# A hybrid decoder layer on one core: block sums of W_out made by GpSimd early in attention, FF1 weights through GpSimd's queue, and the gate's product as one pass

## The chip, the cores and the metric

The kernel runs on one core of a Trainium2 chip. The metric is the device time of one execution in microseconds (us), lower is better. The kernel before took a median of 2267.89 us in three runs (2264.93 to 2271.97).

## The reference

One decoder layer over 2048 tokens of width 1024, in float32:

```
n = RMSNorm(x)
h = x + W_out [ GLA_heads(n) ; DilatedSWA_heads(n) ]
h = h + SqReLU_MLP(RMSNorm(h))          # FF1: 1024 -> 4096, FF2: 4096 -> 1024
y = RMSNorm_final(h)
```

One input projection W_in makes the queries, keys, values and gates of both mixers. GLA is gated linear attention in chunks, with four heads; its forget gate is a low-rank product, log_sigmoid((n W_low) W_2 + b), where n W_low has 16 columns and W_2 is 16x256. The other mixer is windowed attention with strides 1, 4 and 16 (three branches per head, eight heads), whose branch outputs are combined by their softmax denominators.

## The kernel before, in words

**Products.** TensorE has to give float32 results from the faster form fp32r. So each operand is split into a high part that fp32r holds and the rest, and `mm3` (L139 to L142) issues three matmuls: high by high (L140), low by high (L141), high by low (L142). ScalarE makes the high part (L484) and VectorE the low one (L485) in `split`. The large products are done as 2x2 blocks with seven block products in place of eight (numbers j = 1 to 7), so sums and differences of blocks of each operand are needed.

**Stages.** The trace's 2263 us fall into the input projection in two halves of the tokens (to about 520 us), attention (to about 868), the product with W_out (to about 1040), FF1 (to about 1690) and FF2. The order of the instructions on each engine is fixed when the kernel is built: a scheduler lays out TensorE, VectorE, ScalarE and GpSimd by a simulated timeline, and each engine then runs its list in order. In attention, a plan says with which of some 160 units of work a step is issued (`at_unit`).

**The gate.** `gate` (L304) runs 16 times, once per 128 tokens, inside the input projection. It sets a 17x128 tile to one, transposes the 128x16 product `glow` (L309), copies it in (L310) and multiplies by the 17x256 matrix of W_2 and b in full float32 (L312). The trace shows that product as two matmuls of 17x256 each.

**Sums for W_out.** `mix_wo` (L1112) is called four times in the stage of the W_out product, once per pair of row blocks c and c+4. SyncE's queue loads 2 x 512 KB into `wtraw`, GpSimd makes four differences of 128x512 in place (L1118) and each is split by ScalarE and VectorE into `wb`. Beside this, GpSimd and VectorE combine the last branch outputs of attention (L927 to L950); the result goes into `mT` and from there into TensorE's product (L141 with the tile ps_d). `load_wo` (L1103) loads the unmixed blocks through `woraw`.

**FF1 weights.** There are 32 groups (16 weight blocks for each half of the tokens) with seven block products each. `load_w1` (L1346) loads a group of 1024x256 as two halves of 512 KB into one of two buffers `w1raw`; `prep1` (L1356) makes the block sums on VectorE (L1369 to L1373), splits them into `w1comb` and, once a half was read for the last time, asks for that half of the group two further on. These loads stand on SyncE's queue (L1354), as nearly all transfers do. SyncE issues in order, and each of its transfers also waits for the landing of the one eight before it. Around the first groups its queue also holds the transposed rows that go out and come back (hTD, L1254 and L1291), and the stores hD and actD.

**Other names.** `pt` (L878) is ScalarE's copy of transposed probabilities, which TensorE reads in L890; `ar` (L1472) and `bb` (L1267) are ScalarE's copies of transposes that TensorE waits for in the W_out stage; `gla` tiles belong to GLA, whose step has GpSimd products (L1020 to L1025, L1067) and a ScalarE scaling behind L1067 (L1069); `qp` is a query tile that GpSimd reorders and rounds for strided attention (L804). The only transfers on GpSimd's queue are 16 accumulating loads of 512 KB in FF2 (L1698).

## Time and profile before

| | |
|---|---|
| median of three runs | 2267.89 us |
| the profiled execution | 2265.11 us |
| its span in the trace | 2263.3 us |
| mean granted TensorE clock | 0.995 |
| TensorE busy | 2226.8 us |
| VectorE, ScalarE, GpSimd busy | 1696.3, 1249.3, 503.4 us |
| moved by DMA | 482.80 MB |

The trace is of one execution; the profiled time is 1.8 us above its span, for what lies before the first and after the last instruction. "Busy" counts the time in which at least one instruction of the engine runs. A busy TensorE can still run at half its clock; the column PEclk of a table by stage tells that. Queries by stage give the busy time of each engine between two times; the list of waits gives what an engine waited for last; the chain of waits follows the end of the span back from releaser to releaser.

### The profile page before, as it was taken

How to read it: one execution, taken by the hardware profiler on the slowest of the kernel's cores; microseconds unless marked ns; L12 is line 12 of the kernel's file. 1: busy time of each engine (PE TensorE's matmuls, PEld its weight loads, DVE VectorE, ACT ScalarE, POOL GpSimd, SP SyncE). 2: the span in 40 equal slices, each digit the busy share in tenths (PEclk: the TensorE clock that was granted, in tenths of full speed). 3: DMA queues.
4: the chain of work that ended last, by engine and by line, in shares of the span. 5: the costliest groups of instructions: out<-in, count | busy, mean ns of one | idle time of the engine just before them, and what ended most of it. 6: DMA issues, size and time to landing. Idle time of an engine off the chain costs nothing.

```text
span 2263.3 us, 35306 instructions
## 1 busy us (share of the span) xinstructions
PE 2226.8 (98%) x12436; PEld 1924.6 (85%) x12436; DVE 1696.3 (75%) x3172; ACT 1249.3 (55%) x2483; POOL 503.4 (22%) x471
## 2 busy tenths in 40 slices
PE   9999999999999998999899999999999999999998
PEld 8978998899999997888688888888888888888876
DVE  8788878766677678778777778767686796566788
ACT  6665446535877884456555566555555433333435
POOL 1210002025286676100000000000006322032452
PEclk9999999999999999999999999999999999999999
DMA  6457754786667965768645446554479997676775
GB/s 205 133 182 242 249 163 125 219 250 220 208 210 221 296 191 206 256 220 263 212 131 164 130 158 224 168 168 155 139 251 286 316 301 265 216 254 240 258 262 177
DMA packets 363602, 482.80 MB, mean 213 GB/s; under 512 B 20197, under 2 KB 269558, under 8 KB 353184
## 3 DMA queue, kind: packets, MB, share of 16 engines
q1 hardware_dynamic: 358926, 471.89, 64.0%
q0 software_dynamic: 4352, 8.39, 2.1%
q8 instruction: 98, 1.61, 0.3%
q14 instruction: 80, 0.66, 0.1%
q10 hardware_dynamic: 146, 0.27, 0.0%
HBM read 330.74 MB, written 154.44 MB: 214 GB/s over the span
## 4 chain that ended last, share of the span: by engine, by line
PE 86%; DVE 5%; DMA 4%; issue 3%; POOL 1%; ACT 1%; POOLq 0%; SPq 0%; DVEq 0%; ACTq 0%
PE ps_a L141 8%; PE ps_a L142 8%; PE ps_a L140 8%; PE ps_c L140 7%; PE ps_c L142 7%; PE ps_c L141 7%; PE ps_d L141 4%; PE ps_d L142 4%; PE ps_d L140 4%; PE ps_a L890 4%; PE ps_o L142 4%; PE ps_o L140 4%; PE ps_o L141 4%; PE ps_d L871 3%; PE ps_c L853 2%
## 5 line engine op out<-in xcount | busy, mean ns | idle before, releaser
L1649 POOL TENSOR_TENSOR bs<-bs,rb 128x1024 f32<-128x1024 f32 x60 | 177.4, 2964 | 1025.5 <-DMA actD<-ring 781.6
L485 DVE TENSOR_TENSOR cb<-bs,cb 128x1024 fp32r<-128x1024 f32 x104 | 166.5, 1601 | 137.6 <-ACT cb L484 137.6
L484 ACT ACTIVATE cb<-bs 128x1024 fp32r<-128x1024 f32 x104 | 110.3, 1061 | 287.5 <-issue 151.6
L485 DVE TENSOR_TENSOR w1comb<-w1raw,w1comb 128x512 fp32r<-128x512 f32 x224 | 153.3, 686 | 84.2 <-ACT w1comb L484 84.2
L484 ACT ACTIVATE w1comb<-w1raw 128x512 fp32r<-128x512 f32 x224 | 139.7, 625 | 87.7 <-PE ps_a L142 27.2
L862 ACT ACTIVATE pe<-pe,O 128x256 f32<-128x256 f32 (+1 forms) x384 | 158.0, 454 | 53.7 <-DVE O L861 51.3
L890 PE MATMUL ps_a<-v,pt 128*128 128x65 f32 x1200 | 180.8, 255 | 5.6 <-ACT pt L878 5.6
L890 PEld LDWEIGHTS ps_a<-v,pt 128*128 128x128 f32 x1200 | 176.1, 196 | 7.2 <-ACT pt L878 6.0
L871 PE MATMUL ps_d<-ident,pe 128*128 128x128 f32 x600 | 160.7, 282 | 0.0
L861 DVE CUSTOM_DVE_ANT_0 pe<-ps_c,nb 128x256 f32<-128x256 f32 (+1 forms) x384 | 126.5, 361 | 44.4 <-PE ps_d L871 17.7
L284 ACT ACTIVATE wcomb<-wraw 128x512 fp32r<-128x512 f32 (+2 forms) x119 | 90.0, 757 | 98.7 <-PE ps_a L141 35.1
L140 PE MATMUL ps_c<-hb,w1comb 128*128 128x512 f32 x320 | 124.7, 390 | 2.3 <-DVE acc L1443 1.4
L142 PE MATMUL ps_c<-hb,w1comb 128*128 128x512 f32 x320 | 124.5, 389 | 0.0
L141 PE MATMUL ps_c<-hb,w1comb 128*128 128x512 f32 x320 | 124.5, 389 | 0.0
L142 PE MATMUL ps_c<-cb,ca 128*128 128x512 f32 x312 | 121.8, 391 | 0.0
L141 PE MATMUL ps_c<-cb,ca 128*128 128x512 f32 x312 | 121.7, 390 | 0.0
L140 PE MATMUL ps_c<-cb,ca 128*128 128x512 f32 x312 | 121.6, 390 | 0.0
L485 DVE TENSOR_TENSOR ca<-ra,ca 128x1024 fp32r<-128x1024 f32 x84 | 117.4, 1398 | 0.0
L1428 ACT ACTIVATE acc<-acc 128x512 f32<-128x512 f32 x96 | 60.5, 631 | 90.9 <-DVE acc L1443 42.0
L871 PEld LDWEIGHTS ps_d<-ident,pe 128*128 128x128 f32 x600 | 110.2, 188 | 0.3
L349 POOL TENSOR_TENSOR acc<-acc,misc 128x264 f32<-128x264 f32 (+1 forms) x32 | 38.7, 1222 | 313.7 <-DVE acc L348 300.8
L142 PE MATMUL ps_a<-wcomb,tb 128*128 128x256 f32 (+1 forms) x344 | 97.7, 284 | 0.0
(464 smaller groups left out, 7206.4 us busy)
## 6 DMA issues: line engine op xcount, KB each, us to landing
ra<-actD SPq DMA_DIRECT2D x52, 1024.0 KB, 7.7
actD<-ring SPq DMA_DIRECT2D x176, 256.0 KB, 3.3
rb<-w_ff SPq DMA_DIRECT2D x88, 512.0 KB, 5.9
bs<-w_ff SPq DMA_DIRECT2D x72, 512.0 KB, 5.9
w1raw<-w_ff SPq DMA_DIRECT2D x64, 512.0 KB, 4.3
k<-kD SPq DMA_DIRECT2D x16, 1024.0 KB, 8.1
rb<-hTD SPq DMA_DIRECT2D x28, 512.0 KB, 5.9
wraw<-w_in SPq DMA_DIRECT2D x48, 256.0 KB, 3.4
```

The costliest lines, as they stand in the source:

```text
L140: T.matmul(out, sh, mh, start=first, stop=False, **kw)
L141: T.matmul(out, sl, mh, start=False, stop=False, **kw)
L142: T.matmul(out, sh, ml, start=False, stop=last, **kw)
L284: A.activation(hi, src, AF.Copy, scale=sc)
L484: A.activation(hi, src, AF.Copy)
L485: V.tensor_tensor(lo, src, hi.bitcast(F32), op=OP.subtract)
L861: V.tensor_tensor_reduce(p, s, bias, scale=1.0, scalar=BIG, op0=OP.add, op1=OP.min, accum_out=nm)
L862: A.activation(p, p, AF.Exp, bias=nm, scale=-1.0)
L871: T.transpose(pb[:, i * 128:i * 128 + 128], src, ident)
L890: T.matmul(self.b.opsum[:, n % 4], self.pt[:, i * 128:i * 128 + 128], self.b.v[:, blk, cols], start=first, stop=last)
L1428: A.activation(v, v, AF.Relu)
L1649: (engines or ((G,), (V, V))[len(sums) - 1])[e].tensor_tensor(v, v, r, op=OP.add if op == "+" else OP.subtract)
```

## The change

- **The gate** becomes one fp32r matmul. ScalarE writes the rounded `glow` twice (columns 0 to 15 and 33 to 48), VectorE writes the rest into columns 17 to 32, and columns 16 and 49 hold ones; the 128x50 tile is transposed, copied and multiplied by a 50x256 matrix: rows 0 to 16 the rounded weights, 17 to 32 the same again, 33 to 49 what the rounding left of them. That matrix is made once, ahead of the second half, by a ScalarE and a VectorE instruction and a transfer within SBUF.
- To make room, the gain of the first norm lives in `CX` in the first half; the gains and the gate's weights come later through two small DRAM tiles (`gD`, `wD`): three loads at the start go, eight small transfers come after the second weight loads.
- **`sum_wo`** makes the differences of W_out's blocks in attention: for each c two loads of 512 KB into `wtsum`, four GpSimd subtractions and one store of 1 MB to `wtD`, a step per unit from unit 8 on. `mix_wo` then loads 2 x 512 KB of finished differences and only splits them. 4 MB more are loaded and 4 MB more stored than before.
- **`load_w1`** issues on GpSimd's queue.

The diff, with most context left out (a changed line's number after is up to 29 higher):

```diff
@@ -230,9 +230,12 @@
-    misc = slot("misc")
-    gB, gnB, w2b = misc[:, :D], misc[:, D:D + 512], misc[:17, D + 512:D + 768]
-    gTs = [misc[:17, D + 768 + 128 * i:D + 896 + 128 * i] for i in range(2)]
+    misc = slot("misc", FR)
+    gB, gnB = misc[:, :D].bitcast(F32), misc[:, D:D + 512].bitcast(F32)
+    w2b, w2raw = misc[:50, D + 512:D + 768], misc[:50, D + 768:D + 1024]
+    gTs = [w2raw[:, 128 * i:128 * i + 128] for i in range(2)]
+    small = const.tile([128, 96], F32, name="small")
+    lows = [misc[:, 2 * D:2 * D + 50], small[:, :50].bitcast(FR)]
@@ -258,6 +261,7 @@
+    gD, wD = dram.tile([1, D + 512], F32, name="gD"), dram.tile([17, 256], F32, name="wD")
@@ -303,11 +307,13 @@
     def gate(glow, t):
-        gT = gTs[t % 2]
-        V.memset(gT, 1.0)
+        gT, l = gTs[t % 2], lows[t % 2]
+        hi = bass.AP(tensor=l.tensor, offset=l.offset, ap=[*l.ap[:1], [33, 2], [1, 16]])
+        A.activation(hi, glow[:, None, :].to_broadcast([128, 2, 16]), AF.Copy)
+        V.tensor_tensor(l[:, 17:33], glow, l[:, 0:16].bitcast(F32), op=OP.subtract)
         pt = ps("d")
-        T.transpose(pt[:16, :128], glow, ident)
-        V.tensor_copy(gT[:16], pt[:16, :128])
+        T.transpose(pt[:50, :128], l.bitcast(F32), ident)
+        V.tensor_copy(gT, pt[:50, :128])
         pg = ps("d")[:, :256]
         T.matmul(pg, gT, w2b, start=True, stop=True)
@@ -491,13 +497,13 @@
     def x_stat(t):
-        A.activation(CX[:, :D], xs[t], AF.Square, accum_out=ss)
+        A.activation(c12[:, :D], xs[t], AF.Square, accum_out=ss)
     def x_scale(t, cs=slice(0, D)):
-        V.scalar_tensor_tensor(xs[t][:, cs], xs[t][:, cs], X[t], gB[:, cs], op0=OP.mult, op1=OP.mult)
+        V.scalar_tensor_tensor(xs[t][:, cs], xs[t][:, cs], X[t], CX[:, cs], op0=OP.mult, op1=OP.mult)
@@ -609,7 +615,7 @@
         x_load(0, xs[0])
-        g1, one = c11[:1, :D], c12[:1, :128]
+        g1, one = c11[:1, :D], c21[:1, :128]
@@ -621,18 +627,15 @@
-        SP.dma_start(gnB, bcast_row(a["gla_norm_g"], 512))
-        SP.dma_start(w2b[:16], a["gla_gate_w2"].rearrange("o r k -> (o r) k"))
-        SP.dma_start(w2b[16:17], a["gla_gate_b"])
-        V.tensor_copy(gB[:, :512], gp[0])
+        V.tensor_copy(CX[:, :512], gp[0])
-        A.activation(gB[:, 512:], gp[1], AF.Copy)
+        A.activation(CX[:, 512:D], gp[1], AF.Copy)
@@ -678,6 +681,13 @@
                 load_w(1, n, k)
+        SP.dma_start(gD[:, :D], a["attn_norm_g"])
+        SP.dma_start(gD[:, D:], a["gla_norm_g"])
+        SP.dma_start(wD[:16], a["gla_gate_w2"].rearrange("o r k -> (o r) k"))
+        SP.dma_start(wD[16:], a["gla_gate_b"])
+        SP.dma_start(misc[:, :D + 512].bitcast(F32), bcast_row(gD, D + 512))
+        for r, n in ((0, 17), (17, 16), (33, 17)):
+            SP.dma_start(w2raw[r:r + n].bitcast(F32), wD[:n])
@@ -726,6 +736,11 @@
         taken(1, 2)
+    for l in lows:
+        A.activation(l[:, 16:50:33], pair, AF.Copy, scale=0.0, bias=1.0)
+    A.activation(w2b, w2raw.bitcast(F32), AF.Copy)
+    V.tensor_tensor(w2raw, w2raw.bitcast(F32), w2b.bitcast(F32), op=OP.subtract)
+    SP.dma_start(w2b[33:].bitcast(F32), w2raw[33:].bitcast(F32))
@@ -904,8 +919,6 @@
-    small = const.tile([128, 96], F32, name="small")
     def combine_load(pr, half):
@@ -1108,15 +1121,28 @@
+    wtD = dram.tile([4, 128, 2 * D], F32, name="wtD")
+    def sum_wo(c):
+        raw = slot("wtsum")
+        for k in range(2):
+            SP.dma_start(raw[:, D * k:D * k + D], wo[:, c + 4 * k])
+        yield
+        b11, b12, b21, b22 = [raw[:, 512 * k:512 * k + 512] for k in range(4)]
+        for dst, x, y in ((b12, b12, b11), (b22, b22, b12), (b21, b21, b22), (b11, b22, b11)):
+            G.tensor_tensor(dst, x, y, op=OP.subtract)
+            yield
+        issue_later(4, wtD[c], raw[:, :2 * D])
+        yield
     def mix_wo(c):
         raw = slot("wtraw")
-        SP.dma_start(raw[:, :D], wo[:, c])
-        SP.dma_start(raw[:, D:2 * D], wo[:, c + 4])
-        b11, b12, b21, b22 = [raw[:, 512 * k:512 * k + 512] for k in range(4)]
-        for dst, x, y, j in ((b12, b12, b11, 5), (b22, b22, b12, 6), (b21, b21, b22, 4), (b11, b22, b11, 7)):
-            G.tensor_tensor(dst, x, y, op=OP.subtract)
-            split(*block_view(j, c), dst)
+        for k in range(2):
+            SP.dma_start(raw[:, D * k:D * k + D], wtD[c, :, D * k:D * k + D])
+        for k, j in ((1, 5), (3, 6), (2, 4), (0, 7)):
+            split(*block_view(j, c), raw[:, 512 * k:512 * k + 512])
     for part in range(4):
@@ -1203,6 +1229,9 @@
     NU = len(units)
+    sums_wo = [x for c in range(4) for x in [sum_wo(c)] * 6]
+    for n, x in enumerate(sums_wo):
+        at_unit(8 + AHEAD + n, next, x)
@@ -1351,7 +1380,7 @@
             g0 = g % NP * 256
             for k in halves:
-                SP.dma_start(raw1[g % 2][:, 4 * k:4 * k + 4], w1[:, 4 * k:4 * k + 4, g0:g0 + 256])
+                G.dma_start(raw1[g % 2][:, 4 * k:4 * k + 4], w1[:, 4 * k:4 * k + 4, g0:g0 + 256])

```

Three places of the order of instructions follow.

GpSimd in early attention, before (L1020 to L1025 and L1067 are a GLA step's products, `qp` is reordered for the third head; in the trace this is 576 to 592 us):

```order
L1023 TENSOR_TENSOR gla<-gla 64x2x128 [waits DMAHW2_49,Activation_49]
L1023 TENSOR_TENSOR gla<-gla 64x2x128 [waits Pool_49]
L1025 TENSOR_TENSOR gla<-gla 128x2 [waits Pool_49]
L1020 TENSOR_TENSOR gla<-gla 128x256 [waits Activation_49]
L804 COPY qp<-qs 128x512 [waits DMAHW4_49,PE_49]
L804 COPY qp<-qs 128x512 x3
L1067 TENSOR_TENSOR gla<-gla 128x512 [waits Activation_49]
L758 MEMSET v 128x16x2 [waits PE_49]
```

And after (L1134 are the subtractions on `wtsum`, L1080 is what L1067 was, L1036 what L1023 was, L819 what L804 was):

```order
L1134 TENSOR_TENSOR wtsum<-wtsum 128x512
L1036 TENSOR_TENSOR gla<-gla 64x2x128 [waits DMAHW2_49,Activation_49]
L1036 TENSOR_TENSOR gla<-gla 64x2x128 [waits Pool_49]
L1038 TENSOR_TENSOR gla<-gla 128x2 [waits Pool_49]
L1033 TENSOR_TENSOR gla<-gla 128x256 [waits DMAHW3_49,PE_49,Activation_49]
L1134 TENSOR_TENSOR wtsum<-wtsum 128x512 [waits DMAHW3_49,PE_49]
L819 COPY qp<-qs 128x512 [waits DMAHW1_49,PE_49]
L819 COPY qp<-qs 128x512 x3
L1080 TENSOR_TENSOR gla<-gla 128x512 [waits Activation_49]
L773 MEMSET v 128x16x2 [waits DMAHW4_49]
L1134 TENSOR_TENSOR wtsum<-wtsum 128x512 [waits DMAHW5_49,Pool_49]
```

One subtraction with a wait for its load stands ahead of a reordering of `qp` and of the GLA product behind it; twelve others stand shortly ahead of these rows.

GpSimd at the end of attention, before (L948 and L950 are the combination of the last branch outputs, L1118 the subtractions for W_out; 876 to 923 us):

```order
L942 TENSOR_TENSOR gla<-gla 128x8 [waits DVE_49]
L942 TENSOR_TENSOR gla<-gla 128x8 x2
L948 TENSOR_TENSOR O_9446<-O_9446,gla 128x4x128 [waits Pool_49]
L948 TENSOR_TENSOR cmb<-cmb,gla 128x4x128 [waits Pool_49] x2
L950 TENSOR_TENSOR O_9446<-O_9446,cmb 128x4x128 [waits Pool_49] x2
L1118 TENSOR_TENSOR wtraw<-wtraw 128x512 [waits DMAHW6_49,PE_49]
L1118 TENSOR_TENSOR wtraw<-wtraw 128x512 [waits DMAHW7_49,Pool_49]
L1118 TENSOR_TENSOR wtraw<-wtraw 128x512 [waits Pool_49]
L1118 TENSOR_TENSOR wtraw<-wtraw 128x512
L1118 TENSOR_TENSOR wtraw<-wtraw 128x512 [waits DMAHW2_49,Activation_49]
```

And after (L961 and L963 are L948 and L950):

```order
L955 TENSOR_TENSOR gla<-gla 128x8 [waits DVE_49]
L955 TENSOR_TENSOR gla<-gla 128x8 x2
L961 TENSOR_TENSOR O_9507<-O_9507,gla 128x4x128 [waits Pool_49]
L961 TENSOR_TENSOR cmb<-cmb,gla 128x4x128 [waits Pool_49] x2
L963 TENSOR_TENSOR O_9507<-O_9507,cmb 128x4x128 [waits Pool_49] x2
L1383 DMA w1raw<-w_ff 128x4x256 [waits PE_49]
L1383 DMA w1raw<-w_ff 128x4x256
L1383 DMA w1raw<-w_ff 128x4x256 [waits PE_49]
L1383 DMA w1raw<-w_ff 128x4x256
L1383 DMA w1raw<-w_ff 128x4x256 [waits DMASW0_49,DVE_49]
```

Behind the last combination stand no more subtractions, but the loads of FF1 weights, all 64 of them one after the other.

VectorE at the start of FF1, before (`w1raw_11392` is the buffer of the even groups, `w1raw_11541` that of the odd ones; `acc1` and L1443, L1447 are sums of products; L1274 to L1277 serve the second half's norm; L1369 is the first sum of a new group, 1092 to 1107 us):

```order
L1443 TENSOR_TENSOR acc1_11548<-ps_a_11549,acc1_11548 128x512
L485 TENSOR_TENSOR w1comb_11515<-w1raw_11392,w1comb_11515 128x512
L1276 TENSOR_TENSOR xh_11250<-bb_9974,xh_11250 128x512
L1277 TENSOR_TENSOR xh_11250<-xh_11250,bb_9974 128x512
L485 TENSOR_TENSOR w1comb_11515<-w1raw_11541,w1comb_11515 128x512
L1443 TENSOR_TENSOR acc1_11651<-ps_d_11652,acc1_11651 128x512
L1369 TENSOR_TENSOR w1raw_11392<-w1raw_11392 128x4x128
L485 TENSOR_TENSOR w1comb_11516<-w1raw_11392,w1comb_11516 128x512
L1447 TENSOR_TENSOR acc1_11548<-ps_c_11672,xs1_11547 128x512
```

And after (`w1raw_11437` even, `w1raw_11586` odd; L1398 is what L1369 was, L1472 and L1476 what L1443 and L1447 were):

```order
L1472 TENSOR_TENSOR acc1_11593<-ps_a_11594,acc1_11593 128x512
L491 TENSOR_TENSOR w1comb_11560<-w1raw_11437,w1comb_11560 128x512
L1472 TENSOR_TENSOR acc1_11696<-ps_d_11697,acc1_11696 128x512
L491 TENSOR_TENSOR w1comb_11561<-w1raw_11437,w1comb_11561 128x512
L1430 TENSOR_TENSOR ring1_11858<-acc1_11593 128x256 x2
L1398 TENSOR_TENSOR w1raw_11437<-w1raw_11437 128x4x128
L1430 TENSOR_TENSOR ring1_11858<-acc1_11593,ring1_11858 128x256
L1476 TENSOR_TENSOR acc1_11593<-ps_c_11717,xs1_11592 128x512
L491 TENSOR_TENSOR w1comb_11561<-w1raw_11437,w1comb_11561 128x512
L1399 TENSOR_TENSOR w1raw_11437<-w1raw_11437 128x4x128
```

The split of the new group's first block (`w1comb_11516`, after `w1comb_11561`) moves from behind the first sum to ahead of it; the last reading of the even buffer's old contents (`w1comb_11515` and `w1comb_11560` from the even buffer) stays ahead of both.

## The prediction

> **What bounds the kernel now.** The profiled execution took 2265.11 us, 2263.3 of them in the trace, and it is the base of the sum; the median of three runs is 2.8 us above it. Read first is the page's first part, busy time by engine, and then the table by stage (for each stretch: its length, busy time of each engine, granted TensorE clock, DMA share, GB/s).
>
> ```profile
> PE 2226.8 (98%) x12436; PEld 1924.6 (85%) x12436; DVE 1696.3 (75%) x3172; ACT 1249.3 (55%) x2483; POOL 503.4 (22%) x471
> ...
> 57.00:510.00 453.00, 452.62 (x2766) 398.03 (x2765) 349.22 (x548) 238.96 (x468) 52.58 (x45) 1.00 0.64 195
> ...
> 566.00:623.00 57.00, 57.00 (x518) 56.18 (x518) 39.81 (x172) 46.20 (x144) 15.74 (x26) 1.00 0.69 209
> ...
> 850.00:906.00 56.00, 49.51 (x285) 42.55 (x284) 48.98 (x89) 25.44 (x62) 37.01 (x42) 0.94 0.57 201
> ...
> 1076.00:1133.00 57.00, 50.41 (x218) 39.29 (x217) 40.48 (x74) 29.86 (x53) 0.00 (x0) 1.00 0.65 207
> 1133.00:2100.00 967.00, 967.00 (x4268) 800.72 (x4267) 711.43 (x1081) 489.01 (x724) 126.30 (x53) 1.00 0.65 209
> ```
>
> TensorE is the bound: it idles 36.5 us in all, and in the two long stretches 57 to 510 and 1133 to 2100 less than 0.4 us. So an edit pays in two ways only: it takes work off TensorE where it never waits, or it fills one of the holes, of which 850 to 906 (6.5 us) and 1076 to 1133 (6.6 us) are the largest the change can reach. Time saved on another engine elsewhere is worth nothing. What TensorE waited for in 850 to 930, by the list of waits, and then one hole as the chain of waits shows it:
>
> ```profile
> PE ps_d L141 <- DVE mT L485: 3.3, 1, 3.3
> PE ps_a L890 <- ACT pt L878: 3.2, 1, 3.2
> PE ps_c L1337 <- ACT ar L1472: 1.7, 1, 1.7
> ```
>
> ```profile
> 890.27 0.69 PE ps_d L141
> 890.96 0.43 PE ps_d L142
> ...
> 893.52 0.43 PE ps_d L142
> 893.95 0.23 PE ps_d L140
> ```
>
> The second view shows that a long hole costs twice. After the 3.3 us wait the product's matmuls take 0.43 us each, against 0.23 later; eight of them at 0.20 more make 1.6 us. The table's clock of 0.94 in that stage is the same thing.
>
> **The gate.** Before, two full float32 passes; in the chain (a stage where TensorE is always on it) and, for the form the change uses, two consecutive fp32r matmuls of 256 columns on TensorE's timeline:
>
> ```profile
> 112.04 0.62 PE ps_d L312 x2
> ```
>
> ```profile
> 59.73 0.28 PE L141 MATMUL ps_a<-wcomb,tb 128*128 128x256 f32 x1
> 59.85 0.29 PE L142 MATMUL ps_a<-wcomb,tb 128*128 128x256 f32 x1
> ```
>
> Starts lie 0.12 us apart, and the 256 columns are what TensorE passes, whatever the number of rows. One gate falls from 0.62 to 0.12, 16 of them by 16 x 0.50 = 8.0 us. The transpose stays one instruction. The added ScalarE copy of 128x32 and VectorE subtraction of 128x16 lie under TensorE, with VectorE busy 349 of 453 us there; without that cover they would be 32 short instructions of 0.2 to 0.3 us, some 8 us. I take **-8.0**, with ends -7 and -9.5 (the passage into and out of float32 may cost a little too).
>
> The moved gains and the eight small transfers are issued behind the second weight loads, well before the first gate at 112; the start loses three loads. I cost these at 0, hidden under TensorE's work in 57 to 510, with 1 us either way for the start.
>
> **The subtractions leave the W_out stage.** The 3.3 us hole ends when VectorE has combined the last outputs and split `mT`. Its timeline just before, and GpSimd's:
>
> ```profile
> 880.82 0.16 DVE L936 TENSOR_TENSOR gla<-gla,cmb 128x8 f32<-128x8 f32 x1
> 881.02 1.25 DVE L937 TENSOR_TENSOR gla<-gla 128x8 f32<-128x8 f32 x1
> 882.30 1.21 DVE L936 TENSOR_TENSOR gla<-gla,cmb 128x8 f32<-128x8 f32 x1
> ...
> 884.97 0.68 DVE L948 TENSOR_TENSOR O<-O,gla 128x512 f32<-128x512 f32 x1
> 885.57 3.45 DVE L948 TENSOR_TENSOR cmb<-cmb,gla 128x512 f32<-128x512 f32 x2
> ```
>
> ```profile
> 879.57 2.67 POOL L950 TENSOR_TENSOR O<-O,cmb 128x512 f32<-128x512 f32 x2
> 882.19 6.28 POOL L1118 TENSOR_TENSOR wtraw<-wtraw 128x512 f32<-128x512 f32 x4
> ```
>
> The same VectorE instruction (L936) takes 0.16 us at 880.82 and 1.21 at 882.30, and the two products of L948 take 3.45 us where one alone takes 0.68. Each long one overlaps a GpSimd instruction. With the four subtractions of 882.19 to 888.47 gone, VectorE saves 1.21 - 0.16 = 1.05 and 3.45 - 1.36 = 2.09, together 3.1 of the 3.3 us, and the slow matmuls behind the hole go too, since a hole of a few tenths brings none. Full value 3.3 + 1.6 = 4.9. I take **-4.5**; ends 0 (if the combination's own GpSimd instructions now fall there) and -5.2.
>
> The 1.7 us wait for `ar` stands behind the last four splits on ScalarE. GpSimd begins the subtractions when the second half has landed, and ScalarE's last split and its copy follow their end:
>
> ```profile
> 918.15 5.68 POOL L1118 TENSOR_TENSOR wtraw<-wtraw 128x512 f32<-128x512 f32 x3 [0.79 <-DMA wtraw<-w_out]
> ```
>
> ```profile
> 923.86 0.63 ACT L484 ACTIVATE wb<-wtraw 128x512 fp32r<-128x512 f32 x1 [1.06 <-POOL wtraw L1118]
> 924.40 1.55 ACT L1472 ACTIVATE ar<-ps_c 128x512 f32<-128x512 f32 x3
> ```
>
> From that landing, 918.1, four splits of 0.63 would be done by about 920.7, so the wait is over before it begins: **-1.7**, ends 0 and -2. The other hole, behind `pt` (3.2 us), is ScalarE waiting for `woraw`, which the change does not touch. It stays; ScalarE now has four splits ahead of the last `pt`, and I leave 1 us either way in the range.
>
> **The subtractions enter early attention.** GpSimd is idle there for most of the time (15.7 of 57 us busy), and 16 subtractions of 1.3 to 2.2 us are some 28 us. But its list is in order: one subtraction now waits for a load of `wtsum`, and behind it stand a `qp` reordering for the third head and a GLA product that ScalarE's list needs. SyncE's list has become longer by eight loads and four stores, and the stores wait for GpSimd. In the trace of before:
>
> ```profile
> 578.61 3.98 POOL L804 CAST qp<-qs 128x512 fp32r<-128x512 f32 x4
> 583.98 1.28 POOL L1067 TENSOR_TENSOR gla<-gla 128x512 f32<-128x512 f32 x1 [1.38 <-ACT gla L1054]
> ```
>
> ```profile
> 586.23 1.27 ACT L1069 ACTIVATE gla<-gla,stats 128x128 f32<-128x128 f32 x4
> ```
>
> ```profile
> 598.83 0.23 PE L851 MATMUL ps_c<-k,qp 128*128 128x128 f32 x1
> ```
>
> ScalarE uses the GLA product at 586.2, 1 us after it is there; `qp` of the third head is used from 598.8. The order is built for the new place: ScalarE's use stands behind three `pt` copies more than before. What remains is that loads are late in a crowded stretch. I take **+1**; ends 0 and +8 (a wait as long as the 3.3 us hole plus its slow matmuls, 4.9, and one smaller).
>
> **FF1 weights on GpSimd's queue.** From the list of waits of VectorE in 1076 to 1133, the chain, SyncE's timeline and the answers on the two kinds of loads:
>
> ```profile
> DVE w1raw L1369 <- DMA w1raw<-w_ff: 9.0, 3, 6.6
> DVE xh L1261 <- DMA hD<-xh: 4.7, 1, 4.7
> ```
>
> ```profile
> 1093.28 0.68 DVE w1comb L485
> ...
> 1095.37 7.47 DMA w1raw<-w_ff
> 1102.93 0.69 DVE w1raw L1369
> ```
>
> ```profile
> 1094.01 1.27 SPq L1254 DMA_DIRECT2D hTD<-xh  x1
> ```
>
> ```profile
> L1354 SPq DMA_DIRECT2D w1raw<-w_ff x64: 372/373/2469, 1039.2 to 1636.4; - x64
> ...
> DMA to landing us min/median/max: 3.7/4.3/8.5
> ```
>
> ```profile
> L1698 POOL DMA_DIRECT2D sum<-hD x16: 1189/1203/2124, 1729.7 to 1945.6; - x16
> ...
> DMA to landing us min/median/max: 9.1/11.1/19.3
> ```
>
> VectorE's first sum of the third group waits 6.6 us. The old contents of that half were last read by the split that ends at 1093.96; the load then stood behind a store of hTD and was issued at 1095.37. Only 1.4 us of the 9 are the queue; the rest is release and transfer, and the release stays where it was. A transfer from GpSimd's queue costs 1.2 us of issue. If it then lands as fast as SyncE's (7.47 from issue in this crowded place), the gain is 1.4; if it lands as the accumulating ones (9 and more), it is a loss of 1 to 3. The new order brings one product (12 matmuls of 0.23 us, 2.7 us) ahead of the wait, which shortens TensorE's hole behind it. VectorE is otherwise nearly full to 1130, so the later holes of this stage, some 4 us, follow from what it lost here. I take **-2.0**; ends +3 and -5. In steady state a half is asked for every 9.5 us (597 us for 64), and a buffer is read for the last time about one group, 19 us, before it is needed: neither 4.3 nor 11.1 matters. The 64 issues of 1.2 us lie on GpSimd, which does nothing there (0.00 in the table's row of 1076 to 1133).
>
> The Trainium skill, "DMA: Bandwidth & Descriptors", section "SWDGE vs HWDGE vs iDMA", speaks against this part: a plain transfer belongs on SyncE's or ScalarE's queue, GpSimd's being for accumulation, casts and the irregular. "SBUF — State Buffer", the box on the "DVE blocks DMA" trap, gives a case of about 620 ns that became about 3100 while VectorE ran a copy. By that, each load would be some 2.5 us later (an estimate from that page), and the sum -1.2 us smaller at the start only. VectorE's rows in FF1 are TENSOR_TENSOR, for which the same page names no such mode; no run here shows the trap yet.
>
> **The sum**: -8.0 - 4.5 - 1.7 + 1.0 - 2.0 = -15.2, so 2265.1 becomes **2249.9**, say 2250. The best ends give -9.5 - 5.2 - 2 - 5 - 1 = 2242, the worst -7 + 0 + 0 + 8 + 3 + 1 = 2270.
>
> **Rivals.** (1) Only the gate pays: the hole at 886 is refilled by the combination's own GpSimd instructions, FF1's holes stay because release and transfer set them. For it speaks that VectorE's long instruction at 881.02 overlaps L950, not L1118; against it the 6.28 us of L1118 right ahead of the hole. Then -8.0 and a microsecond of early attention: 2258. (2) Early attention stalls: a late `wtsum` holds GpSimd, ScalarE behind it and then TensorE, 5 to 8 us with the slow clock, while the rest comes: 2256. (3) The slower side: loads on GpSimd's queue take longer than the 19 us lead, the accumulating ones having taken up to 19.3. From that point on every one of 30 groups is late by the excess; at 1 us that is +30, minus the 13 us gained elsewhere: 2282. Against it: the accumulating ones themselves have a median of 11.1. (4) The change does not do what it says: the gate's one pass runs at a full float32 pace (0.31 us for one pass), so the gate gains 5 and not 8: 2253, inside the first forecast's width.
>
> **Chances.** The forecast (2243 to 2255) 0.50, rival 1 0.17, rival 2 0.15, rival 3 0.13, others 0.05. The range to leave out 2 in 10 is 2241 to 2270. A measurement of this kernel tells about 0.3%, 6.8 us, from no change. Below 2261 lie the forecast, nearly all of rivals 1 and 2: faster 0.75; the same 0.11, from the ends of rivals 1 and 2; slower 0.14.
>
> **What would show it.** The gate's line with 16 matmuls instead of 32 and TensorE still without holes in 57 to 500; no `mT` wait near 880 and clock 1.00 there; no `ar` wait; a first group's wait in FF1 of 4 to 6 us instead of 6.6; landing times of `w1raw` below 19 us. It is wrong if a wait on `qp`, `k` or `gla` appears between 560 and 620, if `w1raw` lands later than its lead, or if VectorE's long instructions at 881 to 889 keep their length.

## The result, and the profile after

The changed kernel takes **2250.68 us**, the median of four runs (2249.42 to 2255.05), beside 2269.93 for four runs of the kernel before (2264.93 to 2272.35): a ratio of 0.9921, with an interval of 0.9898 to 0.9945. In a later batch the same kernel gave 2247.37 beside 2269.83 (0.9918, 0.9897 to 0.9940). By the ratios it is faster by 18 to 19 us; the forecast was 2250.0, a gain of 15.2 on its base.

The profiled execution was the slowest of the four, 2255.05 us with 2253.2 in the trace; that of before, 2265.11, was close to its kernel's fastest. The pair of profiles differs by 10.1 us only. A second profile of the changed kernel, called after_again below, took 2248.15 (2246.4 in the trace). Part of what lies between the two is the clock, as the experiments show.

Busy time by engine, and the table by stage of the kernel after (columns as in the prediction). From attention on the stretches are cut some 10 us earlier than those of before. Its work moves up by less at first: attention begins 0.7 us earlier, the product with W_out 2.8, and only inside FF1 is it 10.7.

```profile
PE 2223.8 (99%) x12420; PEld 1926.0 (85%) x12420; DVE 1687.0 (75%) x3173; ACT 1256.1 (56%) x2502; POOL 537.0 (24%) x535
```

```profile
57.00:500.00 443.00, 440.40 (x2682) 387.89 (x2681) 342.88 (x545) 240.46 (x483) 36.86 (x38) 1.00 0.64 194
...
553.00:610.00 57.00, 57.00 (x533) 56.41 (x532) 38.35 (x178) 44.38 (x136) 36.03 (x39) 1.00 0.83 286
...
840.00:896.00 56.00, 52.21 (x355) 46.41 (x354) 48.56 (x125) 33.82 (x89) 22.31 (x34) 0.94 0.77 240
...
1066.00:1123.00 57.00, 55.99 (x254) 45.88 (x253) 46.86 (x83) 34.53 (x61) 4.50 (x6) 1.00 0.76 236
1123.00:2090.00 967.00, 966.70 (x4264) 800.09 (x4263) 713.71 (x1081) 491.24 (x724) 167.61 (x107) 1.00 0.66 209
```

TensorE idles 29.4 us where it idled 36.5. The start of FF1 is nearly closed (1.0 us idle, 6.6 before), and the stretch behind 896 is full (57.00 of 57). The end of attention has kept 3.8 us of holes and its clock of 0.94. The stretch 57 to 500, which was full, now has 2.6 us of holes. TensorE's list of waits for 840 to 930 after the change:

```profile
PE ps_a L140 <- DVE O L908: 2.3, 1, 2.3
PE ps_d L140 <- ACT mT L490: 0.6, 1, 0.6
...
PE ps_a L905 <- ACT pt L893: 0.2, 1, 0.2
```

Of the waits of 3.3 (`mT`), 3.2 (`pt`) and 1.7 us (`ar`), 0.6, 0.2 and nothing are left, and a new one of 2.3 has come. Two more new ones lie ahead of 840, in both profiles of the changed kernel. Those of after_again, from 780 on:

```profile
PE ps_a L905 <- DVE pt L895: 2.1, 1, 2.1
PE ps_c L866 <- DVE O L876: 1.6, 1, 1.6
```

Between the 400th score product and W_out's first product on `mcomb` TensorE idles 10.7 us before, 6.9 after and 7.6 in after_again. VectorE's waits in 1060 to 1130, and the rows of the tile `w1raw` (duration in ns as lowest, median, highest, then the landing times):

```profile
...
DVE w1raw L1398 <- DMA w1raw<-w_ff: 3.3, 3, 1.9
...
DVE xh L1290 <- DMA hD<-xh: 0.7, 1, 0.7
```

```profile
L1383 POOL DMA_DIRECT2D w1raw<-w_ff x64: 748/751/987, 1036.5 to 1626.9; - x64
...
DMA to landing us min/median/max: 4.2/5.4/9.1
```

VectorE waits 3.3 us for weights (9.0 before, in the rows that the prediction quotes) and 0.7 for the store of `hD` (4.7 before); what it waits for most is now ScalarE's high parts of `w1comb` (4.6 us in two waits, 1.1 before). The loads land after 5.4 us in the middle and 9.1 at worst.

**Where the time went.** Each profile was cut at the same fixed points of TensorE's own list: the first score product of attention, 100 and 400 of them later, the first product on `mcomb` in W_out, the 300th of FF1, the 500th of FF2, and its last product, some 9 us ahead of the span's end. Microseconds between them, of one execution each:

| | to first score | next 100 | to 400th | to W_out | to FF1's 300th | FF1 and FF2 | rest |
|---|---|---|---|---|---|---|---|
| before | 522.0 | 37.2 | 126.6 | 240.6 | 215.5 | 654.6 | 457.8 |
| after | 521.3 | 38.7 | 129.6 | 234.1 | 207.5 | 655.5 | 457.5 |
| after_again | 519.5 | 33.8 | 129.6 | 234.3 | 207.2 | 655.1 | 458.0 |
| gate_only | 519.8 | 37.5 | 126.6 | 241.4 | 214.1 | 655.1 | 457.6 |
| sums_only | 523.1 | 34.0 | 129.6 | 233.4 | 213.3 | 654.9 | 456.3 |
| w1_only | 523.0 | 35.7 | 126.6 | 241.8 | 210.7 | 656.0 | 457.0 |
| no_subs | 523.7 | 37.2 | 126.6 | 236.4 | 215.7 | 654.6 | 459.1 |
| gate_back | 521.9 | 34.0 | 129.6 | 231.4 | 211.8 | 655.7 | 457.9 |
| sums_back | 521.2 | 33.9 | 126.6 | 241.0 | 211.7 | 655.3 | 458.1 |
| w1_back | 521.1 | 35.5 | 129.6 | 234.3 | 213.8 | 654.9 | 458.9 |
| gate_128 | 521.5 | 33.6 | 129.6 | 233.9 | 208.1 | 654.6 | 459.7 |
| wraw_pool | 530.1 | 35.4 | 129.6 | 232.6 | 211.4 | 655.5 | 453.8 |
| wraw_pool_128 | 525.8 | 33.6 | 129.6 | 233.1 | 207.8 | 656.3 | 453.6 |
| wo_apart | 520.0 | 33.6 | 129.6 | 231.4 | 211.1 | 655.7 | 459.1 |

With the subtractions in attention some TensorE work stands earlier, so "to 400th" is 3.0 longer in all of those kernels and is read together with "to W_out". Before to after_again, that is -2.5 to the first score, -3.4 in early attention, -3.3 to W_out and -8.3 at FF1's start.

### The profile page after: what moved, and what is told of

It is laid out like the page before. It is cut to its first block, busy times and chain, and to the rows that moved or that the text cites. A ratio compares the mean times of both kernels' runs of the same rounds, so it can differ in the third digit from the quotient of the medians.

```text
span 2253.2 us, 35323 instructions
## 1 busy us (share of the span) xinstructions
PE 2223.8 (99%) x12420; PEld 1926.0 (85%) x12420; DVE 1687.0 (75%) x3173; ACT 1256.1 (56%) x2502; POOL 537.0 (24%) x535
## 4 chain that ended last, share of the span: by engine, by line
PE 90%; DVE 4%; issue 2%; DMA 2%; ACT 1%; POOL 0%; POOLq 0%; SPq 0%; ACTq 0%; DVEq 0%
PE ps_a L141 9%; PE ps_a L142 9%; PE ps_a L140 9%; PE ps_c L141 8%; PE ps_c L140 8%; PE ps_c L142 8%; PE ps_d L140 5%; PE ps_d L141 5%; PE ps_d L142 5%; PE ps_a L905 4%; PE ps_o L141 4%; PE ps_o L140 4%; PE ps_o L142 4%; PE ps_d L886 3%; PE ps_c L868 2%
## 5 line engine op out<-in xcount | busy, mean ns | idle before, releaser
L1383 POOL DMA_DIRECT2D w1raw<-w_ff x64 | 48.3, 756 | 698.6 <-DVE w1comb L491 530.7
L355 POOL TENSOR_TENSOR acc<-acc,misc 128x264 f32<-128x264 f32 (+1 forms) x32 | 27.8, 881 | 320.1 <-DVE acc L354 306.7
L819 POOL CAST qp<-qs 128x512 fp32r<-128x512 f32 x64 | 69.2, 1166 | 121.7 <-PE ps_a L141 105.7
```

Of the source, the lines that this page charges most:

```text
L819: G.tensor_copy(dst, src)
```

## The experiments

All parts of before and after are the texts given above; the edits say which of them a kernel has. Microseconds worked out from a ratio are its distance from 1 times 2270.

### Each part alone: gate_only, sums_only, w1_only, and the change again

`gate_only` is the kernel before with the gate's edits (with the moved gains, `gD` and `wD`), `sums_only` with `sum_wo` and the new `mix_wo`, `w1_only` with one word changed:

```diff
-                SP.dma_start(raw1[g % 2][:, 4 * k:4 * k + 4], w1[:, 4 * k:4 * k + 4, g0:g0 + 256])
+                G.dma_start(raw1[g % 2][:, 4 * k:4 * k + 4], w1[:, 4 * k:4 * k + 4, g0:g0 + 256])
```

> The kernel before with the gate's new product, the moved gains and weights, and nothing else. Theory A (the trace of after): a gate costs TensorE 0.51 us instead of 0.82, so 16 of them give -5.0 us, less what new waits in the input projection take (up to +3.4 us in the one profile of after); 2262 to 2266 if before stands at 2268. Theory B (the prediction): 0.12 instead of 0.62, -8 us, 2260.

> The kernel before with the differences of W_out's blocks made in attention, and nothing else. Theory A (the trace of after): the W_out stage gains about 3 to 4 us and early attention loses 1 to 2: -2 us in all. Theory B (the prediction): the mT hole with its slow matmuls and the ar hole go, -6.2, and early attention loses 1: -5 us.

> The kernel before with the 64 loads of FF1 weights on GpSimd's queue, and nothing else. Theory A (the trace of after): TensorE's waits in the first 60 us of FF1 fall from 9.8 to about 3 us by this alone, because SyncE's queue gets free and the loads are issued 0.3 us after the last reading: -6 to -8 us. Theory B (the prediction): the release sets the load, the queue only 1.4 us of it: -2 us. In both the steady stretch of FF1 stays without waits; a landing later than 19 us would show there.

> The kernel after, unchanged, for a second profile. Theory A: the 3.9 us of TensorE waits between 172 and 216 us in the first profile (a run of 2255.05, against 2249.4 to 2250.7 for the others) belong to that execution; here they are gone and the profiled run is near 2250. Theory B: they belong to the change (its small transfers and moved weights); they stand here too.

Measured: gate_only 2260.18 (0.9963, 0.9946 to 0.9979), sums_only 2259.56 (0.9959, 0.9946 to 0.9973), w1_only 2263.07 (0.9971, 0.9958 to 0.9984), after_again 2247.37 (0.9918, 0.9897 to 0.9940). Alone the parts are worth 8.4, 9.3 and 6.6 us, 24.3 together, and the whole 18.6; with intervals of 3 to 5 us either way, that gap isn't settled as a real one.

Each part gains, so rival 1 (only the gate pays) falls. But the totals don't say where. In its own stage gate_only gains 2.2 us (522.0 to 519.8), w1_only 4.8 (215.5 to 210.7), sums_only 4.2 over "to 400th" and "to W_out" (367.2 to 363.0). These are pairs of single executions; the other profiles bear them out. The first stretch takes 521.9 to 523.7 us in the five profiles with the old gate and 519.5 to 521.3 in the six with the new one on 50 rows (wraw_pool, which moves other loads, left out): 2.2 less on average. "To 400th" and "to W_out" take 367.3 to 368.5 in the four that subtract in the W_out stage and 361.0 to 363.9 in the five that do it in attention and are otherwise parts of the change: 4.8 less. FF1's start takes 213.3 to 215.5 in the four of these nine with the loads on SyncE's queue and 207.2 to 211.8 in the other five: 4.4 less.

Most of gate_only's 8.4 us does not show in its profile, which is 2.6 us shorter than that of before: the profiled execution of before was 4.7 us under the median of its 19 runs, that of gate_only 2.3 over its own. Where the slower runs of before lose their time no profile here shows. Part of sums_only's gain lies in stretches that it doesn't touch, and early attention shows one reason. TensorE's row for the same 30 us in three profiles, before, after and after_again:

```profile
515.00:545.00 30.00, 28.70 (x225) 28.27 (x225) 18.98 (x84) 15.85 (x42) 17.12 (x21) 0.89 0.82 279
```

```profile
515.00:545.00 30.00, 28.74 (x213) 28.38 (x212) 18.68 (x82) 15.39 (x41) 17.41 (x21) 0.83 0.85 288
```

```profile
515.00:545.00 30.00, 28.91 (x262) 28.49 (x261) 23.51 (x100) 18.56 (x49) 19.34 (x23) 1.00 0.89 307
```

All three have one hole of 1.1 to 1.3 us between 525 and 528, but the clock granted behind it was 0.89, 0.83 and 1.00: 3.3, 5.1 and 0 us of 30. The last two are one program. So 5 of the 6.8 us between the two profiles of the changed kernel come from this one place, and no edit is credited with a difference there. In all 14 profiles this hole stands there once; behind it the granted clock is 0.5 for 0, 3.4, 6.8 or 10.2 us. The four holes of 0.88 to 1.09 us cost nothing; of the ten of 1.11 to 1.55 us, seven were followed by half the clock.

### The gate's pass on 128 rows: gate_128

The operands are widened to all 128 partitions, with zeros below the 50 rows; nothing else changes.

```diff
+    w2all, gTall = misc[:, D + 512:D + 768], [misc[:, D + 768 + 128 * i:D + 896 + 128 * i] for i in range(2)]
...
-        T.matmul(pg, gT, w2b, start=True, stop=True)
+        T.matmul(pg, gTall[t % 2], w2all, start=True, stop=True)
...
+        A.activation(misc[:, D + 512:2 * D], CX[:, :512], AF.Copy, scale=0.0)
```

> The kernel after with the gate's matmul on 128 rows instead of 50: rows 50 to 127 of both operands hold zeros, written once. Theory A: the pass takes 0.31 us and the neighbours 0.1 more each because it uses part of the rows; with all 128 it passes at 0.12 like its neighbours, so a gate costs 0.12 instead of 0.51 and TensorE's work falls by 16 x 0.39 = 6.2 us, of which VectorE's full list in the input projection takes back up to 3; 2242 to 2245 if after stands at 2248. Theory B: the 0.31 belongs to a lone matmul of 256 columns between others; nothing changes.

Measured: 2249.12 (0.9908, 0.9887 to 0.9929), no different from the change itself. The price of the pass did fall. TensorE's timeline around a gate of the kernel after, and of gate_128 (start, duration, engine, line, tiles; the distance of the starts is what counts):

```profile
115.25 0.39 PE L142 MATMUL ps_o<-tb,wcomb 128*128 128x512 f32 x1
115.57 0.38 PE L318 MATMUL ps_d<-misc 50*128 50x256 f32 x1
115.88 0.50 PE L140 MATMUL ps_o<-tb,wcomb 128*128 128x512 f32 x1
116.21 0.40 PE L141 MATMUL ps_o<-tb,wcomb 128*128 128x512 f32 x1
```

```profile
114.63 0.39 PE L142 MATMUL ps_o<-tb,wcomb 128*128 128x512 f32 x1
114.86 0.28 PE L319 MATMUL ps_d<-misc 128*128 128x256 f32 x1
114.97 0.40 PE L140 MATMUL ps_o<-tb,wcomb 128*128 128x512 f32 x1
115.20 0.40 PE L141 MATMUL ps_o<-tb,wcomb 128*128 128x512 f32 x1
```

On 50 rows the pass takes 0.31 us, and the matmul ahead of it and the one behind are 0.09 and 0.10 longer than their usual 0.23: 0.50 in all. On 128 rows it takes 0.11 and its neighbours nothing. That is 16 x 0.39 = 6 us less work on TensorE, and no gain clear of the scatter is left of it at the end. The stretch's row and TensorE's waits in it, gate_128, and then the waits of after_again:

```profile
57.00:500.00 443.00, 436.22 (x2676) 388.48 (x2675) 343.94 (x544) 239.74 (x483) 37.39 (x38) 1.00 0.63 192
```

```profile
PE ps_c L140 <- ACT wcomb L289: 1.9, 1, 1.9
PE ps_c L141 <- DVE wcomb L291: 1.5, 2, 1.3
...
```

```profile
PE ps_a L141 <- DVE wcomb L290: 1.0, 1, 1.0
PE ps_c L140 <- ACT wcomb L288: 0.9, 1, 0.9
...
```

In this stretch TensorE idles 0.4 us before, 2.6 after (2.1 in after_again) and 6.8 in gate_128: as its own work shrinks, it waits for the weights of W_in that ScalarE and VectorE combine. The stage has a second limit just behind TensorE.

### Taking that second limit away: wraw_pool and wraw_pool_128

Both are the kernel after (the second with the widened pass), with the loads of `wraw` from the third group on issued by GpSimd, as `w1raw` is.

```diff
-            SP.dma_start(raws[n][:, k, :, :w], w_in[:, 4 * k:4 * k + 4, c0 + n * w:c0 + n * w + w])
+            (G if g > 1 else SP).dma_start(raws[n][:, k, :, :w], w_in[:, 4 * k:4 * k + 4, c0 + n * w:c0 + n * w + w])
```

> The kernel after with the loads of W_in (from the third group on) on GpSimd's queue too. Theory A: in the input projection the freed TensorE time is lost because weight loads stand in SyncE's order behind stores of q, k and nTD (TensorE's new waits at 171 and 212, 2.6 us, and VectorE's behind them); on another queue they come earlier and the stage ends 2 to 4 us sooner. Theory B: the loads are asked for only when VectorE has released the buffer, and then take 6 to 7 us in a crowded stretch whatever the queue; the waits stay and the stage ends as before, 0.

> The same with the gate on 128 rows (0.13 instead of 0.51 us of TensorE per gate, 6 us less work). Theory A: with the loads earlier, part of these 6 us shows: 2 to 5 us below the run without the padding. Theory B: VectorE's list in order bounds the stage; no more than 1 us.

Measured: 2258.55 (0.9944, 0.9924 to 0.9963) and 2252.38 (0.9926, 0.9911 to 0.9941). By the ratios the move costs 5 to 6 us. The first stretch is 9 to 11 us longer (530.1 instead of 519.5 to 521.3): TensorE idles 11.5 us in it, 5.9 in after_again, and half clock takes another 3.4. The last stretch is some 4 us shorter (453.8), for a reason that was not looked for. GpSimd's longest waits in the first 520 us of wraw_pool:

```profile
POOL wraw L271 <- DVE wcomb L290: 81.2, 25, 8.7
POOL wraw L271 <- ACT acc L440: 57.8, 5, 14.4
```

Here GpSimd's list isn't empty. A load stands in it at a fixed place and holds back what is behind it, and the other way round. So the same move that gains at FF1's start loses here. That it loses by what else the list holds is argued from these waits, and was not tried by itself. With the shorter pass 4.3 us of the first stretch come back in this slower variant (530.1 to 525.8), so the pass can be worth something, but not in the kernel after. What exactly orders the W_in loads there was not taken further.

### W_out without the subtractions: no_subs, sums_back, wo_apart

`no_subs` is the kernel before without the 16 subtractions for W_out; the raw blocks are split instead, so its product is that of other weights. `sums_back` is the kernel after with the old `mix_wo` and no `sum_wo`. `wo_apart` is the kernel after in which `load_wo` is a generator that splits four units behind its load.

```diff
-            G.tensor_tensor(dst, x, y, op=OP.subtract)
             split(*block_view(j, c), dst)
```

> The kernel before without GpSimd's 16 subtractions for W_out: the raw blocks are split instead, so this part of the computation is left out; loads, splits and products stay. Theory A (contention): VectorE's two products at 885 take 1.4 instead of 3.4 us, the mT hole goes with the slow matmuls behind it, and so does the ar hole: the W_out stage gains 5 to 6.5 us. Theory B: the combination's own GpSimd instructions hold VectorE as long; only the ar hole goes, 2 us.

> The kernel after with GpSimd's subtractions back in the stage of the W_out product (the new gate and the loads on GpSimd's queue stay). Theory A (the trace): the mT hole with its slow matmuls and the ar hole come back, 6 to 7 us in the W_out stage, and early attention does not change: +6 against after, 2254 to 2256. Theory B (the parts taken alone, whose gains add to more than the whole): part of the sums' gain is shared with the others; +3 or less.

> The kernel after with the splits of W_out's unmixed blocks issued four units behind their loads instead of with them. Theory A: the waits of 1.8, 2.3 and 0.9 us at 821, 825 and 850 come from ScalarE and VectorE, which stand in order at a split whose load has not landed; with the split later these go, with the slow matmuls behind them: -3 to -6 us. Theory B: the waits come from VectorE's load of work there, and the scheduler puts the splits at the same place anyway: 0.

Measured: no_subs 2261.64 (0.9961, 0.9946 to 0.9976), sums_back 2258.19 (0.9952, 0.9935 to 0.9968), wo_apart 2251.16 (0.9919, 0.9905 to 0.9934). The row of before that stands behind the prediction's second L936, then VectorE's and GpSimd's timelines at the same place in no_subs, and TensorE's waits in 850 to 930 there:

```profile
883.54 0.17 DVE L937 TENSOR_TENSOR gla<-gla 128x8 f32<-128x8 f32 x1
```

```profile
882.81 0.16 DVE L936 TENSOR_TENSOR gla<-gla,cmb 128x8 f32<-128x8 f32 x1
883.01 1.16 DVE L937 TENSOR_TENSOR gla<-gla 128x8 f32<-128x8 f32 x1
884.20 0.17 DVE L936 TENSOR_TENSOR gla<-gla,cmb 128x8 f32<-128x8 f32 x1
884.41 1.16 DVE L937 TENSOR_TENSOR gla<-gla 128x8 f32<-128x8 f32 x1
...
886.08 0.69 DVE L948 TENSOR_TENSOR O<-O,gla 128x512 f32<-128x512 f32 x1
886.68 1.29 DVE L948 TENSOR_TENSOR cmb<-cmb,gla 128x512 f32<-128x512 f32 x2
```

```profile
882.82 2.72 POOL L950 TENSOR_TENSOR O<-O,cmb 128x512 f32<-128x512 f32 x2
```

```profile
PE ps_a L890 <- ACT pt L878: 2.6, 1, 2.6
PE ps_a L141 <- DVE mT L485: 0.4, 1, 0.4
```

The two products that took 3.45 us beside the subtractions take 1.29 without them, and the 3.3 us wait for `mT` is 0.4. The short instructions are another matter. The second L936 takes 0.17 instead of 1.21, but the L937 behind it takes 1.16 instead of 0.17: the pair saves nothing, because L950 is still there. Each long one ends 0.02 to 0.03 us after a GpSimd instruction does (the last L950 at 885.54, L937 at 885.57), and the next one starts in the gap and is short. What the short ones do save are 0.75 us in three of L942, 0.32 instead of 1.07 together. The `ar` wait of 1.7 us is gone too; the two `pt` waits stay (5.2 us from 780 on, 5.6 before), so what takes them away in the kernel after comes with the new order of the moved sums and not with the missing subtractions. sums_back brings all three waits back, with all else as in the kernel after:

```profile
PE ps_d L141 <- DVE mT L491: 3.6, 1, 3.6
PE ps_a L905 <- ACT pt L893: 2.7, 1, 2.7
PE ps_c L1350 <- ACT ar L1485: 1.3, 1, 1.3
```

That the subtractions' place makes the `mT` and `ar` waits is shown both ways. The Trainium skill, "SBUF — State Buffer", section "Who interferes with whom", says that a VectorE instruction with two SBUF inputs contends with a GpSimd instruction that reads SBUF; these rows agree, and the price is the rest of the GpSimd instruction: some 1 us for a VectorE one of 0.17 as for one of 0.69.

The new hole of the kernel after is in part of the same kind. VectorE's, GpSimd's and TensorE's timelines there:

```profile
868.84 2.37 DVE L961 TENSOR_TENSOR cmb<-cmb,small 128x512 f32<-128x512 f32 x2
871.13 0.42 DVE L908 COPY O<-ps_a 128x260 f32<-128x260 f32 x1
```

```profile
868.33 1.71 POOL L1080 TENSOR_TENSOR gla<-gla 128x512 f32<-128x512 f32 x1
```

```profile
871.60 0.79 PE L140 MATMUL ps_a<-wb,mT 128*128 128x512 f32 x1 [2.29 <-DVE O L908]
872.19 0.63 PE L141 MATMUL ps_a<-wb,mT 128*128 128x512 f32 x1
872.61 0.63 PE L142 MATMUL ps_a<-wb,mT 128*128 128x512 f32 x1
```

Two products that take 1.29 undisturbed take 2.37 beside a GLA product on GpSimd; the copy of `O` behind them in VectorE's list is late, and TensorE waits 2.3 us and then goes on at 0.43 us a matmul. So 1.1 of the 2.3 us are this; the rest is VectorE's list, which has no gap there. wo_apart moves the splits away from that place. Its stretch to W_out is 2.7 us shorter than in the kernel after (231.4 against 234.1), but that is the clock: TensorE idles 6.8 us in it, as in the kernel after (6.9), and loses 3.4 us to the clock instead of 6.8; gate_back, without this edit, takes 231.4 too. FF1's start is 3.6 longer (211.1 against 207.5), and the median is not below that of the change. No version better than the change was found.

### Two parts without the third: gate_back and w1_back

`gate_back` is the kernel after with the old gate, `w1_back` with the `w1raw` loads on SyncE's queue again.

> The kernel after with the gate, the gains and the gate's weights as before (sums in attention and loads on GpSimd's queue stay). Theory A (the trace): the gate gives 5.0 us of TensorE and takes back 2.6 in new waits at 171 and 212: +2 to +5 us against after. Theory B (the prediction): +8.

> The kernel after with the FF1 weight loads back on SyncE's queue (the new gate and the sums in attention stay). Theory A: the queue alone removes the holes of FF1's start; they come back with 5 to 8 us against after. Theory B: most of them had gone with the other two parts already (4.9 us of holes were left with the sums alone, 3.0 in after): +2 to +3.

Measured: gate_back 2253.08 (0.9927, 0.9903 to 0.9951), w1_back 2258.82 (0.9952, 0.9934 to 0.9970). From the whole's 0.9918 to 0.9921, taking the gate back costs 1 to 2 us, taking the queue back 7 to 8, and taking the sums back (sums_back) 7 to 8, with intervals of 4 to 5 us either way. VectorE's waits in 1060 to 1130 of w1_back are close to those of before, on the new kernel:

```profile
DVE w1raw L1398 <- DMA w1raw<-w_ff: 7.0, 3, 5.9
DVE xh L1290 <- DMA hD<-xh: 5.0, 1, 5.0
```

The second wait was not in the prediction's account. SyncE's list in w1_back and VectorE's row behind the store, and both for after_again:

```profile
1070.28 0.92 SPq L1522 DMA_DIRECT2D hD<-xh  x1
1071.29 0.43 SPq L1383 DMA_DIRECT2D w1raw<-w_ff  x1
```

```profile
1077.32 1.28 DVE L1290 SCALAR_TENSOR_TENSOR xh<-xh,stats,gs 128x1024 f32<-128x1024 f32 x1 [4.96 <-DMA hD<-xh]
```

```profile
1066.76 0.58 SPq L1522 DMA_DIRECT2D hD<-xh  x1
```

```profile
1071.76 1.28 DVE L1290 SCALAR_TENSOR_TENSOR xh<-xh,stats,gs 128x1024 f32<-128x1024 f32 x1 [0.90 <-DMA hD<-xh]
```

From issue of the store to VectorE's start it is 7.0 us where a 512 KB load of `w1raw` is issued right behind it on the same queue, and 5.0 where it isn't. The same reading of all 14 profiles gives 6.2 to 7.4 us in the five kernels with the loads on SyncE's queue, and 4.5 to 5.6 in eight of the nine others; the ninth, sums_back, has 6.7 and so doesn't fit. Nor is it that no load shares the transfer engines with the store: in the nine, GpSimd issues a load of the same size within 0.3 us of the store. In the kernel after, with its store at 1073.67:

```profile
1073.71 0.75 POOL L1383 DMA_DIRECT2D w1raw<-w_ff  x1 [21.91 <-DVE w1comb L491]
```

In the five, a store of `hTD` and a load of `rb` also stand just ahead of the store in SyncE's list, in the nine behind it. Which of these makes the store slow was not tried. It isn't the whole wait either: in sums_only the store is as slow (7.4), but VectorE comes to it later and waits only 0.9.

## Why the prediction was right, and where only its sum was

The total came out: 2250.0 forecast, 2250.68 measured, and -15.2 against -18 to -19 by the ratios. That it came so close is in part luck. The gate's term was some 6 us too large and W_out's 1 to 3, FF1's 3 to 4 too small, and the base was one of the faster runs of its kernel.

- **The gate: forecast -8.0 (ends -7 and -9.5), found -2.2 in its stage and 1 to 2 us when taken back.** gate_only's run totals alone (-8.4, interval -12 to -5) would not contradict -8; its profile and the price of the pass do. The step failed twice. "One gate falls from 0.62 to 0.12" took the distance of 128-row matmuls for a 50-row one ("whatever the number of rows"): the pass takes 0.31, as each of the two did before (0.62), so TensorE's work falls by 16 x 0.31 = 5.0 and not 8.0. This is the price that rival 4 named. And "it takes work off TensorE where it never waits" was taken to pay in full: idle time in 57 to 500 rose from 0.4 to 2.6 us. A row with no idle time says that TensorE is the limit, not how far away the next one is. gate_128 shows that it is near: 6 us less work, no gain clear of the scatter.
- **W_out: forecast -4.5 for `mT` and -1.7 for `ar`, found -3.3 to -4.2 for the whole stage in single pairs, -4.8 on average over nine profiles.** Both waits went by the mechanism that was named; no_subs and sums_back show it. Of the 3.1 us that VectorE was to save, the 2.09 of the two products came; the 1.05 of L936 did not, since L937 behind it grew by as much, and 0.75 of L942, which was not counted, made up for it by luck. The two `pt` waits, of which one was to stay, went as well (5.6 to 0.2 us). What the -6.2 left out is what is late next: waits of 2.3, 1.6 and 1.4 to 2.1 us for VectorE's copies of `O` and `pt`, the first beside a GpSimd GLA product, at 871.6, where the old hole stood at 890.3. With them came the slow matmuls that the forecast had counted as gone (0.94 in 840 to 896, as before).
- **Early attention: forecast +1, found about 0.** The 16 subtractions take 1.26 to 1.31 us each and lie between 545 and 597; no wait on `qp`, `k` or `gla` has come in 553 to 610, where TensorE is full (57.00 of 57). Rival 2 falls. The 1.3 us wait on `O` at 527 was there before the change.
- **FF1's queue: forecast -2.0 (ends +3 and -5), found -4.8 alone and -6.3 when taken back (213.8 to 207.5).** The direction was right and the size was off, beyond its best end in the second case. The account had the queue's 1.4 us and the transfer. It left out the store of `hD`, which lands some 2 us sooner in most of the kernels with the loads on GpSimd's queue, for a reason that stays open, and for which VectorE had waited 4.7 us in a row that the prediction itself quotes. Nor is this all: with the loads still on SyncE's queue, the moved sums alone shorten FF1's start by 2.2 us (215.5 to 213.3; TensorE idles 4.6 us in it instead of 8.5). The Trainium skill's "DMA: Bandwidth & Descriptors", "SWDGE vs HWDGE vs iDMA", which puts plain transfers on SyncE's or ScalarE's queue, is half borne out: a load does take longer (5.4 us to landing against 4.3) and its issue too (0.75 against 0.37). It is still the better place here, as w1_only and w1_back show; GpSimd does nothing else there before (0.00 in the row of 1076 to 1133). The 2.5 us by which the prediction had each load later are 1.1 by the medians.
- **Rival 3**, loads later than their lead, had a point of 19 us; the longest landing is 9.1, and TensorE is busy for 966.70 of 967 us from 1123 on.
- **The sum** was made against a profiled execution that was one of its kernel's fastest. The total scatters with the clock: 19 runs of before lie between 2264.1 at a mean clock of 0.996 and 2275.7 at 0.991. With the time lost to the clock taken off each run (its time x (1 - clock)), the median of these 19 is 2256.3, and those of the change's two sets of four runs are 2239.9 and 2238.4: -16.4 and -17.9 from the work and its waits, and the remaining 3 to 5 us of the difference of the medians from the clock. The clock is given to three digits, which leaves 1 us either way in each of these.

## What to carry to other kernels

Where a bound engine's row shows no idle time, ask how near the next limit is before a saving is counted in full: idle time that appears there is the saving that was lost. A load in an in-order list is priced by what it waits for and what stands behind it, not by its own speed, so the same move of queue gained 7 us in one stage and lost 5 to 6 in another. And a stage's own cut between fixed instructions says more of an edit than the total, of which several microseconds are the clock's.

## What the runs showed that was not expected

- A matmul pass with 17 (in float32) or 50 (in fp32r) of 128 rows in use, among full ones, takes 0.31 us for 256 columns, with some 0.1 us more at each edge; the one of 50, padded with zeros to 128 rows, takes 0.11 and nothing at its edges.
- A hole of 1.26 us was followed in one execution by a mean clock of 0.83 over 30 us, and one of 1.09 us in another of the same program by 1.00. The longer holes at this place were followed by half the clock more often, but one of 1.31 (gate_back) was not; what else decides it no row here shows.
- A VectorE instruction of 128x8 with two SBUF inputs took 0.17 us alone and 1.16 to 1.25 beside a GpSimd one, and ended just behind it, while the next one got through at 0.17: the price is that of waiting, not of its size, and one long row less need not be time saved.
- 64 plain loads of 512 KB from GpSimd's queue landed in 4.2 to 9.1 us, where the accumulating ones take a median of 11.1.
